# Two more pairs of column groups on Strassen's scheme, with two units each, in a matmul-bound decoder layer

## The chip, the cores and the metric

The kernel runs on one core of a Trainium2 chip. The time is that of one execution on the device, in microseconds (us). PE is the matmul engine, PEld its weight loads, DVE, ACT and POOL the vector, scalar and GpSimd engines, SP the engine whose queue issues the transfers.

## The reference

One decoder layer for 256 tokens of width 2048, in float32:

```python
h = rmsnorm(x, norm_mix_g)
u = h @ w_in                      # 12288 columns: c, b, xa, za, q, f, iv, og (1024 each), ga, gb (2048 each)
ya = b * conv3(c * xa) * silu(za)
o = hgrn2_chunked(silu(q), (1 - lb) * sigmoid(-f), iv, log_f)
yb = rmsnorm_per_head(o) * silu(og)
m = sigmoid(ga) * (ya @ w_a_out) + sigmoid(gb) * (yb @ w_b_out)
x = x + m @ w_o
x = x + sigmoid(rmsnorm(x) @ w_ple_gate) * (p @ w_ple_proj)
out = rmsnorm(x)
```

## The kernel before

Every projection is cut into groups of 512 output columns, and a group's 2048 input rows into eight chunks of 256. Tokens lie in two tiles of 128. The activations (`hT`, `mT`, `x1T`) stand on PE as stationary operands, split into a high and a low part (`xh`, `xl`), and the weights stream: PE makes three products per pair of tiles (`xh` with `whi`, `xh` with `wlo`, `xl` with `whi`), so a chunk of one group is 12 matmuls of 128x512.

A step is one such chunk. For each step ACT copies the loaded weights (`raw`, 128x1024) to `whi` (line 166) and DVE subtracts that from `raw` to make `wlo` (line 167); both are called the split here. Weights come in units of 1 MB through three `raw` buffers, and splits run three steps ahead of PE into four buffer pairs. In some stages more pairs stand ready: the table `MORE` names, per stage, tiles of other pools that are free then (`inner`: two, `outer`: two, `gates`: one), and `ahead` counts them.

Some groups are computed in pairs. A pair's program is a tuple such as `INNER` or `OUT`: `(0, 4)` is two steps, chunks 4 and 5 of the pair's first group; `(1, 4)` the same of the second; `(2, 3)` chunk 3 of both; `("S", 1)` is a **unit**: chunk 1 of both groups as one 2x2x2 block product by Strassen's scheme, in four steps (parts 0 to 3) of 6, 3, 6 and 6 matmuls. A unit needs sums of the weights, which DVE makes in place in `raw` (`combine_weights`, lines 181, 184 and 185), a split of the 512-wide third sum (part 1, here the half split), and sums of the activations, the forms (`forms`, lines 777 to 785). Its products land in four extra PSUM banks (`s`), and `sums` (line 845 is its `add`) puts these and the four plain banks (`g`) together when the last unit is done, so group 0 of a pair is finished before the pair ends if its own plain chunks stand early in the program.

The order of the groups: four of `w_ple_proj` (PP); for the first half of the columns f, then q with iv as a pair (QV, `FRONT`, 2 units), og, c, xa, za, b; for the second half f, q, then iv with og as a pair (VG, `INNER`, 3 units), c, xa, za, b; four pairs ga and gb (`OPENING` 2 units, `GATES` 4 each), each followed by its groups of `w_a_out` and `w_b_out`; `w_o` as a pair of groups 0 and 1 (OO, `OUT`, 3 units) and groups 2 and 3 alone; `w_ple_gate` as group 0 alone, groups 1 and 2 as a pair (GP, `LATE`, 3 units) and group 3 alone.

Behind its last matmul each group has an epilogue, a generator that `advance()` moves by one yield per step, so its operations stand in the engines' queues between the splits. `ep_f` scales the forget gate's logits, turns them through DRAM and a DVE transpose (line 354), takes two sigmoids, scales them by `oml` and `lbm` in eight 128x256 pieces on DVE (lines 407 and 414), and later takes logarithms on ACT and a scan on DVE (line 434). `ep_o` adds an output group to `x`, turns it, and makes the next operand `x1T` and, for the pair's groups, the gate's forms. `gated` applies the last gate. The scheduler of the build may move matmuls within what the waits allow; the queues of the other engines are in order.

Of the kernel before, what the change touches and what calls it, by code (L numbers as in the profile page):

```python
# [55 lines left out]
def hybrid_kernel(ctx, tc, xT, x, pT, prm, gfin, masks, w_in, w_a, w_b, w_o, w_pg, w_pp, out):  # L56
# [28 lines left out]
    def nm(s):  # L85
        uid[0] += 1
        return f"{s}_{uid[0]}"
# [86 lines left out]
    def combine_weights(pos):  # L174

        b = load(pos).rearrange("p i (k c) -> p (i k) c", k=2)
        pool, tag, n = ("tmp2", "t2", 2) if more(pos) in ("gates", "last") else ("tmp3", "t2", 1)
        if more(pos) in ("inner", "first"):
            pool, tag, n = "tmp1", ("both", "aoff")[unit_of[pos] // 2 % 2], 1
        t2 = half[unit_of[pos]] = pools[pool].tile([P, CW], F32, tag=tag, bufs=n, name=nm("t2"))  # L180
        nc.vector.tensor_tensor(  # L181
            out=b[:, 0:4:3, :], in0=b[:, 0:3:2, :], in1=b[:, 3:4, :].to_broadcast([P, 2, CW]), op=ALU.subtract
        )
        nc.vector.tensor_tensor(out=t2, in0=b[:, 2, :], in1=b[:, 0, :], op=ALU.add)  # L184
        nc.vector.tensor_tensor(out=b[:, 1, :], in0=b[:, 1, :], in1=t2, op=ALU.subtract)
# [27 lines left out]
    for gi, (kind, j, w, g, op, *program) in enumerate(groups):  # L213
# [4 lines left out]
        for n, (u, c) in enumerate(program[0]):  # L218
# [21 lines left out]
    gates, late = of_kind("GG"), of_kind("PG")[0]  # L240

# [11 lines left out]
    last = range(gates[-1] + 1, closing + 1)  # L253
    outer = range(closing + 6, of_kind("O")[-1] + 1)
    tied.append(range(last[0] - 4, outer[-1] + 1))
    inner = [of_kind(kind) for kind in ("QV", "VG")]
    inner = range(inner[0][0] - 3, inner[0][-1] + 1), range(inner[1][0] - 6, inner[1][-1] + 1)

    def more(pos):

        return "gates" if pos in gates else "last" if pos in last else "outer" if pos in outer else "first" if pos in g0 else "inner" if any(pos in at for at in inner) else None

# [132 lines left out]
    def ep_f(j, psum):  # L395
# [9 lines left out]
        for h in range(4):  # L405
            s = slice(h * T, (h + 1) * T)
            nc.vector.tensor_scalar(
                out=sg[:, s], in0=sg[:, s], scalar1=one[:, h : h + 1], scalar2=low[:, h : h + 1],
                op0=ALU.mult, op1=ALU.add,
            )  # L410
        yield
        for h in range(4):
            s = slice(h * T, (h + 1) * T)
            nc.vector.tensor_scalar(
                out=kT[:, s], in0=sn[:, s], scalar1=one[:, h : h + 1], scalar2=None, op0=ALU.mult
            )
        yield
# [406 lines left out]

    def forms_of_m():

        joined = sorted(c for u, c in OUT if u == "S")
        raws = []
# [5 lines left out]
        for j in range(0, len(joined), 2):  # L834
            chunks = joined[j : j + 2]
            r = raws[j // 2].rearrange("p (u k t) -> p u k t", u=2, k=2)[:, : len(chunks)]
            made = lambda: tuple(
                pools["tmp2"].tile([P, 1024], F32R, tag=f"Sx{j}{x}", bufs=1, name=nm("Sm"))[:, : 512 * len(chunks)] for x in "hl"
            )
            yield from forms("mT", made, r, chunks)  # L840
            for _ in range(3):
                yield

    def add(out, x, y):
# [153 lines left out]
    def ep_gates_late(j, e, left):  # L998
        def then(q, g):
            gate = gated(j + q, g, [g[:, A], g[:, B]])  # L1000
            next(gate)
            active.append(gate)
            if q == 0:
                load_projection(3)

# [240 lines left out]
    def ahead(pos):  # L1246

        at, n = more(pos + LEAD), 0
        while n < len(MORE[at]) and more(pos + LEAD + n + 1) == at and (at == "gates" or more(pos + LEAD - 2 * n) == at):
            n += 1  # L1250
# [68 lines left out]
    for pos, (gi, c) in enumerate(steps[:last_group]):  # L1319
        kind, j, w, g, opname, *program = groups[gi]  # L1320
        nch = w.shape[2]
        if kind == "PG" and j == 0 and c == 0:
            close_pool("outer")
# [25 lines left out]
        if pos == FORMS:  # L1349
            active.append(first_forms())  # L1350
            step(active[-1])
        if pos == inner[1][0] - 8:
            third = [
# [19 lines left out]
        if program:  # L1373
# [4 lines left out]
            if c == (min(n for n, (u, _) in enumerate(program) if u == "S"), 0) and kind not in ("G0", "OO"):  # L1378
                active.append({"GG": ep_pair, "GP": ep_gates_late, "QV": ep_inner, "VG": ep_inner}[kind](j, banks, left))
            pair_products(c, program, opname)  # L1380
            ask_ahead()
            if 0 <= pos - TOKENS < 4:
                load_tokens(pos - TOKENS)
            if not joint[pos] or c[1] % 2:
# [14 lines left out]
            if kind == "GP" and c in ((1, 1), (3, 1)):  # L1399
                load_projection(1 + c[0] // 2)  # L1400
            continue
# [14 lines left out]

        if kind == "PG" and j == 0 and c < 2:
            advance()
# [4 lines left out]
        if kind != "PG" or j or c >= 2:  # L1423
            advance()
        if pos == gates[-1] - 9:
            active.append(forms_of_m())
            step(active[-1])
        if kind == "O" and c == 1:
            residual(j)
        if kind == "O" and j == 2 and c == 4:  # L1430
            load_gfin()
        if kind == "PG" and c == 4:
            load_projection(j)
        if c == nch - 1:
# [106 lines left out]
```

## Time and profile before

| what | us |
|---|---|
| median of 3 runs | 808.21 (807.93 to 808.41) |
| the profiled execution | 809.07 |
| its span, first to last instruction | 807.3 |
| PE busy in it | 798.0 |
| DVE busy in it | 685.1 |
| ACT busy in it | 492.1 |

The granted clock of PE is 0.996 on average. A matmul's row lasts longer than the distance to the next row's start, since matmuls are pipelined; what one costs is read from the starts. "Splits run ahead" is read by comparing the end of a `wlo` row with the start of the first matmul that reads it.

### The profile page before, as it was taken

How to read it: one execution, taken by the hardware profiler on the slowest of the kernel's cores; microseconds unless marked ns; L12 is line 12 of the kernel's file. 1: busy time of each engine (PE TensorE's matmuls, PEld its weight loads, DVE VectorE, ACT ScalarE, POOL GpSimd, SP SyncE). 2: the span in 40 equal slices, each digit the busy share in tenths (PEclk: the TensorE clock that was granted, in tenths of full speed). 3: DMA queues.
4: the chain of work that ended last, by engine and by line, in shares of the span. 5: the costliest groups of instructions: out<-in, count | busy, mean ns of one | idle time of the engine just before them, and what ended most of it. 6: DMA issues, size and time to landing. Idle time of an engine off the chain costs nothing.

```text
span 807.3 us, 11113 instructions
## 1 busy us (share of the span) xinstructions
PE 798.0 (99%) x4169; PEld 662.3 (82%) x4169; DVE 685.1 (85%) x798; ACT 492.1 (61%) x662; POOL 95.4 (12%) x74
## 2 busy tenths in 40 slices
PE   9999999999999999999999999999999999999995
PEld 7888888888888888888888888888888888887885
DVE  5968897966779987978998998998998988859995
ACT  6967565575656665586674564564565556746562
POOL 0000145300000054300001000000100000002032
PEclk9999999999999999999999999999999999999998
DMA  9899855747676755667584775775875669877542
GB/s 345 295 335 319 268 174 203 237 167 241 240 261 190 261 183 201 209 211 257 189 307 158 227 275 171 239 264 179 275 266 196 208 246 348 327 236 281 205 173 104
DMA packets 50309, 191.20 MB, mean 237 GB/s; under 512 B 5712, under 2 KB 15184, under 8 KB 36304
## 3 DMA queue, kind: packets, MB, share of 16 engines
q1 hardware_dynamic: 50112, 190.24, 68.4%
q8 instruction: 32, 0.52, 0.2%
q10 hardware_dynamic: 144, 0.26, 0.1%
q14 instruction: 21, 0.17, 0.1%
HBM read 175.80 MB, written 14.68 MB: 236 GB/s over the span
## 4 chain that ended last, share of the span: by engine, by line
PE 82%; DVE 10%; issue 2%; DMA 2%; ACT 2%; SPq 0%; POOL 0%; ACTq 0%; POOLq 0%; DVEq 0%
PE g L1258 48%; PE g L1280 25%; PE s L1280 6%; DVE wlo L167 5%; DMA raw<-in_w_pg 2%; ACT whi L166 1%; DVE raw L181 1%; DMA raw<-in_w_o 1%; PE s L1258 1%; PE s L504 1%; DVE t L845 1%; PE s L1131 1%; DVE t L184 1%; DVE t L1017 0%; DVE t L354 0%
## 5 line engine op out<-in xcount | busy, mean ns | idle before, releaser
L167 DVE TENSOR_TENSOR wlo<-raw,whi 128x1024 fp32r<-128x1024 f32 (+1 forms) x320 | 390.2, 1243 | 92.2 <-ACT whi L166 89.4
L166 ACT ACTIVATE whi<-raw 128x1024 fp32r<-128x1024 f32 (+1 forms) x320 | 325.8, 1047 | 175.8 <-PE g L1258 98.3
L1258 PE MATMUL g<-whi,xl 128*128 128x512 f32 (+1 forms) x464 | 177.1, 382 | 0.3 <-DVE xl L311 0.3
L1258 PE MATMUL g<-whi,xh 128*128 128x512 f32 (+1 forms) x464 | 177.4, 383 | 0.0
L1258 PE MATMUL g<-wlo,xh 128*128 128x512 f32 (+1 forms) x464 | 177.1, 382 | 0.0
L1280 PE MATMUL g<-whi,xl 128*128 128x512 f32 x316 | 122.9, 389 | 0.0
L1280 PE MATMUL g<-wlo,xh 128*128 128x512 f32 x316 | 122.9, 389 | 0.0
L1280 PE MATMUL g<-whi,xh 128*128 128x512 f32 x316 | 122.6, 389 | 0.0
L1258 PEld LDWEIGHTS g<-whi,xl 128*128 128x128 f32 x464 | 87.2, 188 | 17.6 <-DVE xl L311 0.8
L1258 PEld LDWEIGHTS g<-whi,xh 128*128 128x128 f32 x464 | 87.2, 188 | 17.0 <-ACT xh L310 0.3
L1258 PEld LDWEIGHTS g<-wlo,xh 128*128 128x128 f32 x464 | 87.3, 188 | 16.8
L166 ACT ACTIVATE whi<-t 128x512 fp32r<-128x512 f32 x25 | 15.8, 632 | 92.1 <-DVE t L184 92.1
L1280 PEld LDWEIGHTS g<-whi,xl 128*128 128x128 f32 x316 | 59.3, 188 | 12.4
L1280 PEld LDWEIGHTS g<-whi,xh 128*128 128x128 f32 x316 | 59.3, 188 | 12.3
L1280 PEld LDWEIGHTS g<-wlo,xh 128*128 128x128 f32 x316 | 59.3, 188 | 12.3
L927 POOL TENSOR_TENSOR t<-ga,gb 128x512 f32<-128x512 f32 x6 | 10.6, 1790 | 188.0 <-issue 118.1
L181 DVE TENSOR_TENSOR raw<-raw 128x1024 f32<-128x1024 f32 x25 | 31.5, 1261 | 0.6
L1258 PE MATMUL g<-whi,yaTh 128*128 128x512 f32 (+1 forms) x74 | 28.2, 388 | 0.0
L1258 PE MATMUL g<-wlo,yaTh 128*128 128x512 f32 (+1 forms) x74 | 27.9, 383 | 0.0
L1258 PE MATMUL g<-whi,yaTl 128*128 128x512 f32 (+1 forms) x74 | 27.9, 383 | 0.0
L1258 PE MATMUL g<-whi,mh 128*128 128x512 f32 x64 | 24.8, 391 | 0.1
L1258 PE MATMUL g<-whi,ml 128*128 128x512 f32 x64 | 24.9, 389 | 0.0
(309 smaller groups left out, 1117.0 us busy)
## 6 DMA issues: line engine op xcount, KB each, us to landing
raw<-in_w_in SPq DMA_DIRECT2D x68, 1024.0 KB, 5.0
raw<-in_w_in SPq DMA_DIRECT2D x37, 512.0 KB, 5.1
raw<-in_w_o SPq DMA_DIRECT2D x12, 1024.0 KB, 6.5
raw<-in_w_pg SPq DMA_DIRECT2D x12, 1024.0 KB, 6.4
raw<-in_w_in SPq DMA_DIRECT2D x38, 256.0 KB, 5.1
turn<-t SPq DMA_DIRECT2D x72, 128.0 KB, 2.8
t<-turn SPq DMA_DIRECT2D x18, 512.0 KB, 5.2
raw<-in_w_a SPq DMA_DIRECT2D x8, 1024.0 KB, 5.6
```

The source lines that it names most:

```text
L166: a = nc.scalar.activation(out=hi[:, s], in_=src[:, s], func=AF.Copy)
L167: v = nc.vector.tensor_tensor(out=lo[:, s], in0=src[:, s], in1=hi[:, s].bitcast(F32), op=ALU.subtract)
L181: nc.vector.tensor_tensor(out=b[:, 0:4:3, :], in0=b[:, 0:3:2, :], in1=b[:, 3:4, :].to_broadcast([P, 2, CW]), op=ALU.subtract)
L184: nc.vector.tensor_tensor(out=t2, in0=b[:, 2, :], in1=b[:, 0, :], op=ALU.add)
L504: nc.tensor.matmul(heads(bk)[r, h, c if at is None else slice(at, at + 32)], key(h)[:, r], query(h)[:, c], start=True, stop=True, tile_pos ...
L845: nc.vector.tensor_tensor(out=out, in0=x, in1=y, op=ALU.add)
L927: (nc.vector if j == 3 else nc.gpsimd).tensor_tensor(out=spread(m, t), in0=blocks(ga[:, s]), in1=blocks(gb[:, s]), op=ALU.add)
L1131: nc.tensor.matmul(wb[:m, :n], *ones, start=True, stop=True)
L1258: nc.tensor.matmul(psum, a, b, start=first and n == 0, stop=last and n == 2)
L1280: nc.tensor.matmul(banks[name], x, y[:, s], start=k == total[name] and i == 0, stop=k == 1 and i == 2)
```

## The change

Four things change in the order of work, and some places follow.

- Second half: f and q become a pair (FQ, `SECOND`, units on chunks 0 and 1). Its forms are those that QV made. The epilogue is `ep_second`.
- `w_o`: groups 2 and 3 become a pair (`CLOSE`, units on chunks 0 and 1). Its forms are made again from `m`, which is read back from DRAM (`forms_of_m`, called a second time with the pool `outer`).
- `w_ple_gate`: the pair is groups 0 and 1 instead of 1 and 2, with a new `LATE`; group 2 is alone.
- `ep_f` makes its eight scalings on ACT instead of DVE, in both halves.
- Buffers and order: VG gets three extra pairs (`wide`) instead of two, FQ two (`inner`), the output pair one (`outer`) instead of two; the stretches in which splits keep their place among the other operations (`tied`) now hold VG and reach to the gate's last unit; loads of x, of the final gain and of the kept projections move with their groups.

```diff
+SECOND = (0, 2), (0, 4), ("S", 0), (0, 6), ("S", 1), (1, 2), (1, 4), (1, 6)
+CLOSE = (0, 2), (0, 4), (0, 6), ("S", 0), (1, 2), ("S", 1), (1, 4), (1, 6)
-LATE = (0, 4), ("S", 0), (0, 6), ("S", 1), (2, 3), ("S", 2), (1, 4), (1, 6)
+LATE = ("S", 0), (2, 3), ("S", 1), (0, 4), ("S", 2), (1, 4), (0, 6), (1, 6)
...
-        elif (kind, j) in (("iv", 0), ("og", 1)):
+        elif (kind, j) == ("f", 1):
+            groups.append(("FQ", j, w_in, n, "hT", SECOND))
+        elif (kind, j) in (("iv", 0), ("og", 1), ("q", 1)):
             continue
...
-    groups += [("OO", 0, w_o, 0, "mT", OUT), ("O", 2, w_o, 2, "mT"), ("O", 3, w_o, 3, "mT")]
-    groups += [("PG", 0, w_pg, 0, "x1T"), ("GP", 1, w_pg, 1, "x1T", LATE), ("PG", 3, w_pg, 3, "x1T")]
+    groups += [("OO", 0, w_o, 0, "mT", OUT), ("O", 2, w_o, 2, "mT", CLOSE)]
+    groups += [("GP", 0, w_pg, 0, "x1T", LATE), ("PG", 2, w_pg, 2, "x1T"), ("PG", 3, w_pg, 3, "x1T")]
...
-        "outer": ((("outer", "whi0"), ("outer", "wlo0")), (("outer", "whi1"), ("outer", "wlo1"))),
+        "outer": ((("outer", "whi"), ("outer", "wlo")),),
...
+        "wide": (
+            (("tmp1", "X"), ("tmp1", "X")), (("tmp1", "a"), ("tmp1", "y")), (("tmp1", "og"), ("tmp1", "cv")),
+        ),
...
-    outer = range(closing + 6, of_kind("O")[-1] + 1)
-    tied.append(range(last[0] - 4, outer[-1] + 1))
+    outer = range(closing + 5, of_kind("O")[-1] + 1)
+    tied.append(range(last[0] - 4, last_unit("GP", LATE) + 3))
     inner = [of_kind(kind) for kind in ("QV", "VG")]
-    inner = range(inner[0][0] - 3, inner[0][-1] + 1), range(inner[1][0] - 6, inner[1][-1] + 1)
+    wide = range(inner[1][0] - 4, inner[1][-1] + 1)
+    inner = range(inner[0][0] - 3, inner[0][-1] + 1), range(of_kind("FQ")[0] - 2, wide[0])
+    tied.append(wide)
...
-            nc.vector.tensor_scalar(
-                out=sg[:, s], in0=sg[:, s], scalar1=one[:, h : h + 1], scalar2=low[:, h : h + 1],
-                op0=ALU.mult, op1=ALU.add,
+            nc.scalar.activation(
+                out=sg[:, s], in_=sg[:, s], func=AF.Identity, scale=one[:, h : h + 1], bias=low[:, h : h + 1]
             )
...
-            nc.vector.tensor_scalar(
-                out=kT[:, s], in0=sn[:, s], scalar1=one[:, h : h + 1], scalar2=None, op0=ALU.mult
-            )
+            nc.scalar.activation(out=kT[:, s], in_=sn[:, s], func=AF.Identity, scale=one[:, h : h + 1])
...
+    def ep_second(j, e, left):
+
+        def then(q, g):
+            after = (ep_q if q else ep_f)(j, [g[:, A], g[:, B]])
+            next(after)
+            active.append(after)
+
+        yield from sums(e, left, lambda: (t4(), t4()), then)
...
             if pos == closing:
                 finish()
                 third_part()
                 state["x1T"] = operand(big, "x", KT)
                 active.append(ep_out(j, banks, left))
+                step(active[-1])
+                active.append(forms_of_m(sorted(c for u, c in CLOSE if u == "S"), homes_of_m("outer", "Sm")))
                 step(active[-1])
...
+            if kind == "O" and c in ((0, 1), (1, 1)):
+                residual(j + c[0])
+            if kind == "O" and c == (2, 1):
+                load_gfin()
```

DVE's queue where the output groups end and the gate begins, before: the first five splits of the gate's group 0 (`raw_6100`, `raw_6158`, `raw_6237`), with what group 1 and group 2 of the output still had to do (`So1l` is a form, `xl` a part of `x1T`).

```order
L167 TENSOR_TENSOR wlo_6222<-raw_6100,whi_6221 128x1024
L785 TENSOR_TENSOR So1l_6206<-t_1100_6160,So1h_6205 128x512
L167 TENSOR_TENSOR wlo_6240<-raw_6100,whi_6239 128x1024
L167 TENSOR_TENSOR wlo_6256<-raw_6158,whi_6255 128x1024
L354 STREAM_TRANSPOSE t_1103_6183<-t_1089_6102 128x4x8x32
L845 TENSOR_TENSOR xs<-xs,g_6116 128x512
L311 SCALAR_TENSOR_TENSOR xl_5826<-t_1103_6183,prm_t,xh_5825 128x256 x4
L845 TENSOR_TENSOR xs<-xs,g_6117 128x512
L167 TENSOR_TENSOR wlo_6289<-raw_6158,whi_6288 128x1024
L167 TENSOR_TENSOR wlo_6311<-raw_6237,whi_6310 128x1024
```

The same place after: the first unit of the gate's pair (`raw_6221`), between the sums of the output pair (line 853 is `add` there, 169 the split, 183 to 187 the combination).

```order
L169 TENSOR_TENSOR wlo_6292<-raw_6221,whi_6291 128x1024
L853 TENSOR_TENSOR t_1130_6235<-t_1130_6235,s_6146 128x1024
L853 TENSOR_TENSOR xs<-xs,t_1129_6234 128x512
L183 TENSOR_TENSOR raw_6221<-raw_6221 128x2x512
L186 TENSOR_TENSOR t_1142_6295<-raw_6221 128x512
L187 TENSOR_TENSOR raw_6221<-raw_6221,t_1142_6295 128x512
L169 TENSOR_TENSOR wlo_6320<-t_1142_6295,whi_6319 128x512
L169 TENSOR_TENSOR wlo_6336<-raw_6221,whi_6335 128x1024
L853 TENSOR_TENSOR t_1130_6235<-t_1130_6235,g_6159 128x512
L853 TENSOR_TENSOR t_1130_6235<-t_1130_6235,g_6174 128x512
L169 TENSOR_TENSOR wlo_6369<-raw_6221,whi_6368 128x1024
```

What moved: the unit that used to come a whole plain group later now stands directly behind the output pair, among that pair's last sums.

ACT's queue around the sigmoids of the second half's forget gate, before: they stand in the value and output gate's first unit (`raw_2152`), with no scalings.

```order
L166 ACTIVATE whi_2210<-raw_2152 128x1024
L400 ACTIVATE t_367_2208<-t_366_2206 128x1024
L402 ACTIVATE t_366_2206<-t_366_2206 128x1024
L166 ACTIVATE whi_2240<-t_370_2214 128x512
L166 ACTIVATE whi_2260<-raw_2152 128x1024
```

After: they stand in that pair's second unit (`raw_2264`), with the query's sigmoids (line 379) and the eight scalings (416 and 422) ahead of the half split's copy.

```order
L168 ACTIVATE whi_2366<-raw_2264 128x1024
L409 ACTIVATE t_393_2304<-t_392_2302 128x1024
L379 ACTIVATE t_399_2327<-t_363_2141,r1r_615 128x512 x2
L411 ACTIVATE t_392_2302<-t_392_2302 128x1024
L416 ACTIVATE t_393_2304<-t_393_2304,lc_54_330,lc_55_331 128x256 x4
L422 ACTIVATE kT_2340<-t_392_2302,lc_55_331 128x256 x4
L168 ACTIVATE whi_2385<-t_408_2370 128x512
```

What moved: everything that the forget gate still needs from ACT before its logarithms now stands between the first copy of that unit and its second.

More of the change, by code (lines that the diff above doesn't have):

```diff
@@ L177, in combine_weights @@
         pool, tag, n = ("tmp2", "t2", 2) if more(pos) in ("gates", "last") else ("tmp3", "t2", 1)
-        if more(pos) in ("inner", "first"):
+        if more(pos) in ("inner", "wide", "first"):
             pool, tag, n = "tmp1", ("both", "aoff")[unit_of[pos] // 2 % 2], 1
@@ L239, in hybrid_kernel @@
     of_kind = lambda *kinds: [pos for pos, (gi, c) in enumerate(steps) if groups[gi][0] in kinds]
-    gates, late = of_kind("GG"), of_kind("PG")[0]
+    gates, late = of_kind("GG"), of_kind("GP")[0]
     def last_unit(kind, program):
@@ L823, in forms_of_x, with forms_of_m @@
             yield
-    def forms_of_m():
-        joined = sorted(c for u, c in OUT if u == "S")
+    def forms_of_m(joined, made):
         raws = []
@@ L836, in forms_of_m, with homes_of_m @@
             r = raws[j // 2].rearrange("p (u k t) -> p u k t", u=2, k=2)[:, : len(chunks)]
[L837 to L840, printed above, removed]
+            yield from forms("mT", lambda: tuple(z[:, : 512 * len(chunks)] for z in made(j)), r, chunks)
             for _ in range(3):
                 yield
+    def homes_of_m(pool, tag):
+        return lambda j: tuple(
+            pools[pool].tile([P, 1024], F32R, tag=tag.format(j) + x, bufs=1, name=nm("Sm")) for x in "hl"
+        )
     def add(out, x, y):
@@ L1248, in ahead @@
         at, n = more(pos + LEAD), 0
-        while n < len(MORE[at]) and more(pos + LEAD + n + 1) == at and (at == "gates" or more(pos + LEAD - 2 * n) == at):
+        while n < len(MORE[at]) and more(pos + LEAD + n + 1) == at and (
+            at == "gates" or more(pos + LEAD - 2 * n) == at or at == "wide" and n < 2
+        ):
             n += 1
@@ L1321, in hybrid_kernel @@
         nch = w.shape[2]
-        if kind == "PG" and j == 0 and c == 0:
+        if kind == "GP" and c == (0, 0):
             close_pool("outer")
@@ L1351, in hybrid_kernel @@
             step(active[-1])
-        if pos == inner[1][0] - 8:
+        if pos == wide[0] - 10:
             third = [
@@ L1383, in hybrid_kernel @@
                 load_tokens(pos - TOKENS)
-            if not joint[pos] or c[1] % 2:
+            if (not joint[pos] or c[1] % 2) and (kind, c[0]) != ("GP", 0):
                 advance()
@@ L1414, in hybrid_kernel @@
                         )
-        if kind == "PG" and j == 0 and c < 2:
-            advance()
         if pos >= FIRST:
@@ L1422, in hybrid_kernel @@
             load_tokens(pos - TOKENS)
-        if kind != "PG" or j or c >= 2:
-            advance()
+        advance()
         if pos == gates[-1] - 9:
-            active.append(forms_of_m())
+            active.append(forms_of_m(sorted(c for u, c in OUT if u == "S"), homes_of_m("tmp2", "Sx{}")))
             step(active[-1])
[L1428 to L1433, printed above, removed]
+        if kind == "PG" and c in (3, 6):
+            load_projection(j + c // 6)
         if c == nch - 1:
```

10 lines of the change are left out of this document (5 added, 5 removed).

## The prediction

> **What bounds the kernel now.** I read the page's busy times first, then PE's waits, then the timeline, which shows what one matmul costs.
>
> ```profile
> span 807.3 us, 11113 instructions
> PE 798.0 (99%) x4169; PEld 662.3 (82%) x4169; DVE 685.1 (85%) x798; ACT 492.1 (61%) x662; POOL 95.4 (12%) x74
> ...
> PE s L1131 <- PEq L1530: 0.8, 1, 0.8
> PE g L1258 <- DVE xl L311: 0.3, 1, 0.3
> ...
> 668.67 0.39 PE L1258 MATMUL g<-whi,mh 128*128 128x512 f32 x1
> 668.89 0.39 PE L1258 MATMUL g<-wlo,mh 128*128 128x512 f32 x1
> 669.12 0.39 PE L1258 MATMUL g<-whi,ml 128*128 128x512 f32 x1
> 669.58 0.50 PE L1258 MATMUL g<-whi,mh 128*128 128x512 f32 x1
> ...
> 732.04 0.40 PE L1280 MATMUL g<-whi,xh 128*128 128x512 f32 x1
> 732.79 0.73 PE L1258 MATMUL g<-whi,xl 128*128 128x512 f32 x2 [0.35 <-DVE xl L311]
> ```
>
> PE is busy 99% and its named waits come to 1.1 us: PE is the bound, almost everywhere. A row lasts 0.39 us, but the next one starts 0.22 to 0.23 us after it, so a matmul is worth **0.2267 us** of time, not 0.39. Where starts lie further apart, PE waited: 0.23 us at 669 and 0.52 us at 732. With some 0.4 us in smaller gaps beside these two I count 1.2 us of waits between 668 and 733. DVE, at 85%, is the nearest rival, and it isn't even over the stages:
>
> ```profile
> 196.40:238.60 42.20, 42.20 (x188) 34.94 (x187) 30.38 (x35) 23.55 (x28) 0.11 (x1) 1.00 0.81 280
> 238.60:281.70 43.10, 43.07 (x190) 35.38 (x189) 40.43 (x49) 28.22 (x33) 0.53 (x1) 1.00 0.61 207
> 620.00:668.70 48.70, 48.70 (x217) 40.32 (x216) 45.35 (x51) 25.68 (x28) 0.00 (x0) 1.00 0.64 218
> 668.70:712.50 43.80, 43.73 (x193) 35.92 (x192) 33.02 (x41) 29.01 (x45) 0.00 (x0) 1.00 0.93 337
> 712.50:776.60 64.10, 63.75 (x280) 52.21 (x280) 56.30 (x63) 40.60 (x56) 7.71 (x3) 1.00 0.68 238
> ```
>
> The columns are stretch, length, then busy time of PE, weight loads, DVE, ACT, POOL. The stages are forget and query of the second half; value and output gate; output groups 0 and 1; output groups 2 and 3; the gate's groups 0 to 2. Stages with Strassen units hold DVE at 88 to 94%; the plain stages (72% and 75%) are where it gets ahead again. The change makes the plain ones Strassen too.
>
> **What it removes.** A unit makes 21 matmuls where a plain chunk of two groups makes 24. Four more units save 12 x 0.2267 = **2.72 us**. The waits at 669 and 730 to 733 belong to orders that go (a single output group behind the pair; the gate's group 0 needing the last output group at once), so up to 1.2 us go with them.
>
> **What a unit costs DVE.** From the stage of value and output gate:
>
> ```profile
> 263.61 1.22 DVE L181 TENSOR_TENSOR raw<-raw 128x1024 f32<-128x1024 f32 x1
> 264.87 0.69 DVE L184 TENSOR_TENSOR t<-raw 128x512 f32<-128x512 f32 x1
> 265.59 0.69 DVE L185 TENSOR_TENSOR raw<-raw,t 128x512 f32<-128x512 f32 x1
> 266.34 0.69 DVE L167 TENSOR_TENSOR wlo<-t,whi 128x512 fp32r<-128x512 f32 x1
> 267.50 5.76 DVE L167 TENSOR_TENSOR wlo<-raw,whi 128x1024 fp32r<-128x1024 f32 x5 [0.46 <-ACT whi L166]
> ...
> 664.95 0.68 DVE L845 TENSOR_TENSOR t<-t,s 128x512 f32<-128x512 f32 x1
> 670.04 1.21 DVE L845 TENSOR_TENSOR t<-t,s 128x1024 f32<-128x1024 f32 x1
> ```
>
> Start to start, the combination is 2.73 us (263.61 to 266.34), a half split 0.60, a whole split 1.14 (five in 5.76, the last one's tail off). A unit is 2.73 + 0.60 + 3 x 1.14 = 6.75 us of DVE for 21 x 0.2267 = 4.76 us of PE; the plain chunk is 2.28 for 5.44. So each new unit adds 4.5 us to DVE and takes 0.68 from PE. A new pair also adds its sums, six adds at 0.60 and one at 1.13: 4.7 us.
>
> **Output pair and the gate's pair.** Now three stages with units follow each other (3, 2 and 3 units) with nothing plain between. Take DVE's queue of the new order from behind the split of the output pair's fourth step to the last split of the gate's step (0, 4). Its kinds, counted in that queue:
>
> ```profile
> 667.71 1.22 DVE L167 TENSOR_TENSOR wlo<-raw,whi 128x1024 fp32r<-128x1024 f32 x1
> ...
> 683.14 1.24 DVE L354 STREAM_TRANSPOSE t<-t 128x1024 f32<-128x1024 f32 x1
> ...
> 685.76 0.42 DVE L780 TENSOR_TENSOR t<-t 128x256 f32<-128x256 f32 x1 [0.27 <-ACT t L963]
> 686.16 0.42 DVE L777 SCALAR_TENSOR_TENSOR t<-t 128x256 f32<-128x256 f32 x1
> ...
> 714.13 1.68 DVE L311 SCALAR_TENSOR_TENSOR xl<-t,prm_t,xh 128x256 fp32r<-128x256 f32 x4
> ```
>
> 24 whole splits 27.3; 4 half splits 2.4; 4 combinations 10.9; 19 adds of 512 at 0.60 11.4; two of 1024 2.3; forms of m (four small ones of 0.34 to 0.45, one whole) 2.6; and for the three first output groups transposes (1.16 each), splits of x1 and its forms 4.9 + 3.7 + 2.9. Sum **68.4 us**. The row at 667.71 is the split at which the count starts; it ends at 668.9, so DVE ends at 737.3 if it never waits. PE, from 668.67, reaches that split after 186 + 21 + 24 + 21 + 12 = 264 matmuls, 59.9 us: at 728.5. DVE is 8.7 us late, and PE waits at least that long: it has no other split to use. In the old order DVE was busy 33 us in the first 44 of these.
>
> Gates in the queue add to it. The split before the sums waits for a transfer, an ACT copy and a buffer that PE frees (1.2 us); the forms wait for ACT's gains, 0.3 in the row at 685.76 and about 1.5 where splits of ACT stand behind them; behind each half split ACT must copy first, 0.46 in the row at 267.50, four times 1.8; and a combination, a transpose and four splits of x1 come right after that stretch (1.4). That makes about 6, or 15 in all. Bounds 8.7 and 15; I take **13.5**, nearer to the upper end, since every gate has its row.
>
> The moved transfers (m's 512 KB read again, the 1 MB of x for groups 2 and 3 sooner, the projections' reads) stand before weights on SP's queue; each is 1.5 to 3 us of the 337 GB/s that the fourth window shows. They hide behind DVE's lateness; without that cover the weights of the first unit would be the later ones by 1.5 us. One outer buffer pair less is in the 1.2 us above.
>
> **Forget and query, then value and output gate.** DVE gets 2 x 4.5 + 4.7 = 13.7 us, and the eight scalings that go to ACT take about 2.4 from it (four each in the L407 and L414 rows below). It had 11.8 + 2.7 = 14.5 us idle in the two windows, so DVE alone just fits. ACT does not:
>
> ```profile
> 235.75 1.06 ACT L400 ACTIVATE t<-t 128x1024 f32<-128x1024 f32 x1 [1.00 <-DMA raw<-in_w_in]
> ...
> 241.31 1.24 ACT L370 ACTIVATE t<-g,r1r 128x512 f32<-128x512 f32 x2
> ...
> 243.52 1.28 ACT L424 ACT_TABLE_LOAD   x1
> ...
> 205.75 1.69 ACT L310 ACTIVATE ybTh<-t,prm_t 128x256 fp32r<-128x256 f32 x4
> ...
> 77.91 1.38 DVE L407 TENSOR_SCALAR t<-t,lc,lc 128x256 f32<-128x256 f32 x4 [0.37 <-ACT t L400]
> ...
> 241.09 1.14 DVE L414 TENSOR_SCALAR kT<-t,lc 128x256 f32<-128x256 f32 x4
> ```
>
> In the new order two sigmoids (2.0), the query's two (1.2) and the eight scalings (2 x 1.65, by the L310 row) stand on ACT directly ahead of the copy of the half split of the second unit: 6.5 us. Counted from FQ's first matmul, the split that opens FQ's second unit ends at 16.2: PE frees its buffer's predecessor at 11, one split and ACT's four gains of yb follow, then DVE's four splits of yb. From there to the transpose that releases the sigmoids DVE's queue holds 35.6 us (16 whole splits, two combinations, two half splits with their 0.46, the sums, two transposes, four others), so the sigmoids start at 52.7. PE wants the half split after 261 matmuls, at 59.2; with ACT's 6.5 and its copy it comes 0.5 late. The copies behind it, then the table load and the logarithms (2.4), then the scan, a combination and a transpose on DVE make it up to 5.4 by the third unit. Bounds 0 (DVE alone) and 5.4; I take **4**. In the first half the same block lies where splits are over 2 us ahead, and I cost it at nothing; without that cover it would be 1 us.
>
> ```profile
> 651.70 0.63 ACT L166 ACTIVATE whi<-t 128x512 fp32r<-128x512 f32 x1 [4.26 <-DVE t L184]
> 652.43 5.80 ACT L166 ACTIVATE whi<-raw 128x1024 fp32r<-128x1024 f32 x6
> ```
>
> ACT sat 4.26 us before a half split while six copies stood behind it. [...] Could ACT pass a blocked copy, this stage's term would be 0 and not 4.
>
> **The sum.** The profiled execution took 809.07 us, its span 807.3. 809.07 - 2.7 - 1.2 + 13.5 + 4 = 822.7. The median of the runs is 0.86 lower than the profiled one: **822 us**.
>
> **Rivals.**
> - **Only DVE's bare sum counts**: ACT's block finds its 0.5 us, and the gates are hidden in each other. 809.07 - 3.9 + 8.7 - 0.86 = 813. For it: PE's new order uses the high halves of two or three steps before the low ones, which bridges short waits. Against it: low halves are what is late. 0.22.
> - **Faster: DVE keeps up.** 808.2 - 3.9 = 804.3. It decides in favour of the change when all new waits stay under 3.9 us, so DVE's 68.4 us would have to shrink below 64, some 6%. For it: DVE's total over 620 to 776.6 was 134.7 of 156.6 us and would be 154, which fits if the work could be spread. Against it: the queue puts it in front, and DVE's rows repeat to a few per cent. 0.07; and 0.03 for a tie.
> - **PE's clock falls too.** Single waits of up to 3 us come close together in the gate's first two units. In the trace the clock stays 1.00 through waits of 0.5 us and is 0.60 in the last slice, where PE is idle 7 us. If it fell twice for some 3 us, at half rate, 3 us more: 825, and with all gates 828. 0.10. [...]
>
> **How the numbers follow.** The forecast, both stages late by their gates, gives 817 to 825.5 and has 0.58; the others 0.22, 0.10, 0.07 and 0.03. The range of 8 in 10 goes from 811.5, below the bare sum, to 828. About 0.2% (1.6 us) can be told from no change here. Slower 0.90, within 0.03, faster 0.07.
>
> **What would show it.** PE's matmul count falls by 12 and its starts stay 0.227 us apart inside steps. PE's wait list names DVE (low halves) and ACT, with over 10 us in the stretch from the output pair's second unit to the gate's second, and a few in the value stage's second and third unit; DVE is at 95% or more from the output pair's first unit to the gate's step (0, 4). It would be wrong if DVE idles in that stretch, if PE's waits there sum to under 8 us, or if new waits stand elsewhere, above all on transfers of weights.

## The result, and the profile after

The changed kernel takes **831.89 us** (median of 4 runs, 831.03 to 832.56) beside 808.31 us (807.93 to 808.67) for the kernel before: ratio 1.0291, 95% interval 1.0273 to 1.0309. It is slower by 23.6 us. The forecast was 822, with a range up to 828: the sign was right, the size was not.

The page of the changed kernel, busy times. The profiled execution took 832.56 us.

```profile
span 830.6 us, 11170 instructions
PE 805.5 (97%) x4156; PEld 659.9 (79%) x4157; DVE 709.3 (85%) x821; ACT 506.2 (61%) x689; POOL 90.6 (11%) x74
```

PE's waits in the changed kernel, with what ended each (columns: who waits, for what, us in total, times, longest):

```profile
PE s L1297 <- ACT whi L168: 8.1, 6, 2.3
PE g L1297 <- ACT whi L168: 2.2, 7, 0.9
PE g L1275 <- DVE t L853: 2.0, 1, 2.0
PE g L1297 <- DVE wlo L169: 1.7, 3, 0.9
PE s L1297 <- DVE wlo L169: 1.6, 5, 0.7
```

Most waits end with an ACT copy (`whi`, line 168), not with DVE. That is often the last link only: at the output pair's second unit the copy of the half split itself waits for the combination on DVE (3.53 us in this row):

```profile
706.09 0.63 ACT L168 ACTIVATE whi<-t 128x512 fp32r<-128x512 f32 x1 [3.53 <-DVE t L186]
```

Windows tell more: the length of a stretch less its matmuls at 0.2267 us is what PE waited in it.

```profile
254.00:276.00 22.00, 18.11 (x70) 12.01 (x69) 16.08 (x17) 15.96 (x23) 0.53 (x1) 1.00 0.43 143
700.00:716.00 16.00, 11.07 (x40) 6.68 (x39) 14.25 (x17) 10.57 (x15) 0.00 (x0) 1.00 0.56 208
716.00:750.00 34.00, 29.50 (x111) 22.41 (x110) 32.77 (x43) 20.12 (x32) 0.70 (x1) 0.90 0.65 217
774.00:780.00 6.00, 4.05 (x18) 3.03 (x17) 4.87 (x6) 5.31 (x7) 0.00 (x0) 1.00 0.85 317
```

The stretches are the second and third unit of value and output gate (22 - 70 x 0.2267 = 6.1 us of waits), the second unit of the output pair (6.9), the first two units of the gate's pair (8.8) and the step behind that pair (1.9). DVE is busy 96% of the third stretch, 89% of the second and only 73% of the first. The third one's clock, 0.90, is another thing that was new.

I also summed, for both traces, by how much starts of matmuls lie further apart than 0.2267 us (gaps over 0.3 us). That gives the terms of the prediction as they came:

| term | predicted | measured |
|---|---|---|
| 12 matmuls fewer | -2.7 | -2.7 |
| waits of before that go | -1.2 | -0.6 |
| value and output gate | +4 | +6.1 |
| output pair's second unit to the gate's second | +13.5 | +16.2 |
| behind the gate's pair | 0 | +2.2 |
| forget gate of the first half | 0 | +0.5 |
| third units of output groups 0 and 1 and of the gate | 0 | +1.1 |
| sum | +13.6 | +22.8 (spans: +23.3) |

Some 3 us of the 16.2 are not waits but matmuls that start 0.43 us apart, at a granted clock of 0.50.

### The profile page after: what moved, and what is told of

It reads as the page before. It is cut to its first block, busy times and chain, and to the rows that moved or that the text cites. A ratio compares the mean times of both kernels' runs of the same rounds, so it can differ in the third digit from the quotient of the medians.

```text
span 830.6 us, 11170 instructions
## 1 busy us (share of the span) xinstructions
PE 805.5 (97%) x4156; PEld 659.9 (79%) x4157; DVE 709.3 (85%) x821; ACT 506.2 (61%) x689; POOL 90.6 (11%) x74
## 4 chain that ended last, share of the span: by engine, by line
PE 73%; DVE 13%; ACT 4%; issue 4%; DMA 4%; SPq 0%; ACTq 0%; POOLq 0%; POOL 0%; DVEq 0%
PE g L1275 42%; PE g L1297 23%; DVE wlo L169 6%; PE s L1297 5%; ACT whi L168 3%; DVE raw L183 1%; DMA raw<-in_w_pg 1%; DMA raw<-in_w_o 1%; DVE t L853 1%; DVE t L363 1%; DVE t L186 1%; DMA raw<-in_w_in 1%; PE s L1275 1%; PE s L510 1%; PE s L1146 1%
## 5 line engine op out<-in xcount | busy, mean ns | idle before, releaser
L169 DVE TENSOR_TENSOR wlo<-raw,whi 128x1024 fp32r<-128x1024 f32 (+1 forms) x324 | 397.5, 1253 | 78.0 <-ACT whi L168 75.2
L1275 PE MATMUL g<-whi,xh 128*128 128x512 f32 (+1 forms) x400 | 152.7, 382 | 2.0 <-DVE t L853 2.0
L1275 PE MATMUL g<-wlo,xh 128*128 128x512 f32 (+1 forms) x400 | 152.5, 381 | 0.0
L1275 PE MATMUL g<-whi,xl 128*128 128x512 f32 (+1 forms) x400 | 152.1, 381 | 0.0
L1297 PE MATMUL g<-whi,xh 128*128 128x512 f32 x368 | 143.2, 391 | 1.3 <-ACT whi L168 1.3
L1297 PE MATMUL g<-wlo,xh 128*128 128x512 f32 x368 | 143.6, 390 | 0.0
L1297 PE MATMUL g<-whi,xl 128*128 128x512 f32 x368 | 143.4, 390 | 0.0
L1297 PE MATMUL g<-wlo,mh 128*128 128x512 f32 x98 | 38.3, 390 | 0.5 <-DVE wlo L169 0.5
L1297 PE MATMUL g<-whi,mh 128*128 128x512 f32 x98 | 38.0, 392 | 0.7 <-ACT whi L168 0.4
L1297 PE MATMUL g<-whi,ml 128*128 128x512 f32 x98 | 38.0, 390 | 0.0
```

The source lines that it names most:

```text
L169: v = nc.vector.tensor_tensor(out=lo[:, s], in0=src[:, s], in1=hi[:, s].bitcast(F32), op=ALU.subtract)
L1275: nc.tensor.matmul(psum, a, b, start=first and n == 0, stop=last and n == 2)
L1297: nc.tensor.matmul(banks[name], x, y[:, s], start=k == total[name] and i == 0, stop=k == 1 and i == 2)
```

## The experiments

Every ratio is against the kernel before, run beside it on the same chip. Medians of before were 808.1 to 808.8.

### The parts by themselves

`part_fq` has of the diff what concerns f and q of the second half, with `ep_f` and the buffers of that stage. `part_out_gate` is the changed kernel without it. `part_out` keeps of that only the output pair (old `LATE`, group 0 of the gate alone), `part_gate` only the gate's new pair. In short:

```diff
 part_out_gate and the next two:
-        elif (kind, j) == ("f", 1):
-            groups.append(("FQ", j, w_in, n, "hT", SECOND))
 part_out, and part_fq:
-    groups += [("GP", 0, w_pg, 0, "x1T", LATE), ("PG", 2, w_pg, 2, "x1T"), ("PG", 3, w_pg, 3, "x1T")]
+    groups += [("PG", 0, w_pg, 0, "x1T"), ("GP", 1, w_pg, 1, "x1T", LATE), ("PG", 3, w_pg, 3, "x1T")]
 part_gate and part_fq:
-    groups += [("OO", 0, w_o, 0, "mT", OUT), ("O", 2, w_o, 2, "mT", CLOSE)]
+    groups += [("OO", 0, w_o, 0, "mT", OUT), ("O", 2, w_o, 2, "mT"), ("O", 3, w_o, 3, "mT")]
```

> The kernel before with the first part of the change alone: forget and query of the second half as a pair, the eight scalings on ACT, the extra buffers of that stage; output groups and gate as before. Stage theory (each stage pays for its own lateness, and the parts add up): in the changed kernel's trace this part costs 6.1 us of waits in the value and output gate and 0.6 in the first half, and saves 6 matmuls x 0.2267 = 1.4; so 808.3 + 5.3 = 813.6. Rival (the stage only looks late because the later stages hold it up, or the other way round): the waits in the value stage are gone, 807 to 808.

> The changed kernel without that part: forget and query plain, scalings on DVE; output groups 2 and 3 a pair, gate pair of groups 0 and 1. Stage theory: waits 0.5 + 0.6 + 7.1 + 4.7 + 4.3 + 0.6 in the output groups and the gate, 2.2 behind the gate's pair, less 1.2 that before had there and 6 matmuls (1.4): 808.3 + 17.4 = 825.7, and with the first part's +5.3 the sum is the whole change, +22.7 against 23.6 measured. Rival: the parts share their cost, sum off by more than 2.

> The kernel before with the output pair of groups 2 and 3 alone; the gate in its old order (group 0 plain, then the pair of 1 and 2). Volume theory (DVE's work of the output pair has to be done before the pair's second unit, whatever follows): the 7.1 us of waits at that unit stay, the plain gate group behind takes the rest; 808.3 + 7.1 + 0.7 - 0.7 = 815.4. Rival, adjacency (only three stages of units in a row are too much; either alone has a plain stage behind it to catch up): 808 to 810.

> The kernel before with the gate's pair on groups 0 and 1 alone; output groups 2 and 3 plain. The plain groups before it let DVE get ahead, but the last group's sums, transposes and splits of x1 fall into the pair's first units. Volume theory: half of the 9.0 us in the gate's units was backlog of the output pair, half is the last output group's epilogue; 4.5, plus 2.2 behind the pair, less 0.8: 808.3 + 5.9 = 814. Adjacency: only the 2.2 behind the pair stays: 808 to 810.

| kernel | median us (range) | ratio, 95% interval |
|---|---|---|
| part_fq | 814.05 (812.95 to 814.26) | 1.0065 (1.0053 to 1.0077) |
| part_out_gate | 823.45 (822.77 to 824.43) | 1.0186 (1.0173 to 1.0199) |
| part_out | 821.31 (820.83 to 822.10) | 1.0163 (1.0150 to 1.0176) |
| part_gate | 817.28 (812.82 to 819.27) | 1.0104 (1.0082 to 1.0125) |

The first part costs 5.9 us, the second 15.3; together 21.2 of 23.6. The parts nearly add up; what is missing, 2.4 us, is just beyond the 2 us that the rival of `part_out_gate` asked for. 1.7 of it is one place: the wait behind the gate's pair was 0.57 us without the first part and 2.23 with it. Both theories failed on `part_out` and on `part_gate`. The second unit of `part_out` lost nearly what it loses in the changed kernel (13 us with 31 matmuls in a window of its trace: 6.0 beside 6.9), so adjacency is not the cause there. But the plain gate group behind it then stood still, for a reason that neither named. PE's rows of `part_out`:

```profile
727.19 0.39 PE L1277 MATMUL g<-whi,xl 128*128 128x512 f32 x1
732.89 0.79 PE L1277 MATMUL g<-whi,xh 128*128 128x512 f32 x1 [5.31 <-ACT xh L316]
...
734.40 0.63 PE L1277 MATMUL g<-whi,xh 128*128 128x512 f32 x1
734.83 0.63 PE L1277 MATMUL g<-wlo,xh 128*128 128x512 f32 x1
```

A pair finishes both its groups at its end, so x1 of groups 2 and 3 comes late, and a plain gate group wants it from its fifth chunk on: one wait of 5.3 us. The rows behind it start 0.427 us apart, not 0.227. The gate's new order, which asks for groups 2 and 3 last, removes this wait and pays for it in its own units; by itself it costs 9.1 us, beside the output pair only 2.1. In the trace of `part_gate` (815.41 us) the first unit lost 4.4 us, 1.4 of them to starts 0.43 us apart, and the group behind the pair 2.6; its slower executions, up to 819.27 us, have no trace.

### Forget gate: which engine, or which place

`scal_dve` puts the scalings of `ep_f` back on DVE in the changed kernel. `fq_lag` is `part_fq` with the transpose eight yields later, and the first half's scalings on DVE.

```diff
 fq_lag:
-        sn = yield from turned(fl, 4 if j else 6)
+        sn = yield from turned(fl, 12 if j else 6)
```

> The changed kernel with the eight scalings back on DVE, nothing else. Order theory (what stands on ACT directly ahead of the half split's copy sets the wait): 3.7 us of ACT leave the block between the sigmoids and that copy, DVE stood idle 3.7 and 2.1 us there anyway; the value stage's waits fall from 6.1 to about 3, the first half's 0.6 goes: 832 - 3.5 = 828.5. Rival, DVE's volume: 2.4 us more for DVE in a stage that is late, 832 to 834.

> The kernel before with the forget and query pair alone (as part_fq), with the transpose of the second half's forget gate eight yields later, so that sigmoids, scalings, logarithms and scan stand behind the splits of the third unit of value and output gate; the first half's scalings back on DVE. The work of each engine is that of part_fq. Order theory (the 6.4 us of waits come from this block standing inside the second and third unit, whichever engine it is on): they fall to under 1 us, and the 6 saved matmuls show: 808.1 - 1.4 + 0.5 = 807.2. Volume theory (DVE and ACT have too much to do in this stage): the waits come back behind the third unit or in the next group: 811 to 814.

`scal_dve` took 832.93 us (829.08 to 834.40), ratio 1.0306 (1.0289 to 1.0323): not told apart from the changed kernel. In its trace the first half's waits went, as expected, but those of the value stage fell only from 6.4 to 5.3 us, so the expectation that this block costs less on DVE failed. `fq_lag` took **807.51 us** (807.05 to 808.27, 11 runs), ratio 0.9981 (0.9972 to 0.9990): faster than before, and by the 0.2% that six matmuls are worth. Some 0.7 of the 6.5 us between `part_fq` and `fq_lag` are the first half's waits, which are gone with its scalings on DVE. The stage in `part_fq`, then in `fq_lag`:

```profile
254.00:276.00 22.00, 18.10 (x69) 12.02 (x69) 15.94 (x17) 15.96 (x23) 0.53 (x1) 1.00 0.45 144
```

```profile
236.00:282.00 46.00, 46.00 (x205) 38.09 (x204) 41.35 (x43) 32.37 (x42) 1.55 (x4) 1.00 0.68 230
```

205 matmuls at 0.2267 fill the 46 us: no wait is left in it, and 0.5 us stands just behind it, at 282.4, in a plain step. The work that DVE and ACT have to do for this block is the same. ACT's queue in the changed kernel shows what had stood in the way:

```profile
250.08 1.06 ACT L409 ACTIVATE t<-t 128x1024 f32<-128x1024 f32 x1 [4.16 <-DVE t L363]
251.05 1.32 ACT L379 ACTIVATE t<-t,r1r 128x512 f32<-128x512 f32 x2
252.27 1.04 ACT L411 ACTIVATE t<-t 128x1024 f32<-128x1024 f32 x1
253.22 2.06 ACT L416 ACTIVATE t<-t,lc,lc 128x256 f32<-128x256 f32 x4
255.19 1.69 ACT L422 ACTIVATE kT<-t,lc 128x256 f32<-128x256 f32 x4
256.79 0.61 ACT L168 ACTIVATE whi<-t 128x512 fp32r<-128x512 f32 x1
...
259.32 1.28 ACT L430 ACT_TABLE_LOAD   x1
...
261.77 2.94 ACT L168 ACTIVATE whi<-raw 128x1024 fp32r<-128x1024 f32 x3
```

The half split's copy at 256.79 is behind 6.7 us of the forget gate, the copies at 261.77 behind 2.4 us more, and DVE's splits wait for each. In `fq_lag` the forget gate's rows stand behind ACT's copies for the third unit, from 267.68 on, ahead of those of plain chunks.

### DVE's volume from the output pair to the gate

Three kernels change DVE's work in this stretch, or its place. `less_sums` and `short_comb` leave work out, as their expectations say.

```diff
 late_turn:
-        turn = turned(x1, 6 if j == 1 else 2)
+        turn = turned(x1, 6 if j == 1 else 8 if j == 0 else 2)
 less_sums, for groups 0 and 1 (sums of the pair, adds to x):
-        add(gb[:, A], gb[:, A], e[6])
-        add(both, both, e[5]...)
-        add(gb[:, A], gb[:, A], e[0, 1])
-        add(gb[:, B], gb[:, B], e[1, 1])
-            add(d, d, psum[t])
 short_comb, in combine_weights:
+        if pos < of_kind("O")[0]:
             nc.vector.tensor_tensor(out=b[:, 0:4:3, :], ...)
```

> The changed kernel with the transpose of output group 0 six yields later, so that its transpose, forms and low parts (5.5 us of DVE) stand behind the splits of the output pair's second unit and not ahead of its combination. DVE's work up to the gate's second unit is the same. Volume theory (PE's waits from 700 to 750 us are DVE's queue up to the gate's units, 72.8 us against 59.9 us of PE): the 7.1 us at the output pair's second unit fall to 2 or 3, what is gone comes back at the gate's first unit; 831 to 833. Local theory: 5 us less, 827.

> The changed kernel, with part of the sums of output groups 0 and 1 left out (four adds of their pair sums, the one over both tiles among them, and the four adds to x), so that group 0 and 1 of the output are not what the reference has: 5.3 us less for DVE, all of it 15 us and more ahead of the output pair's second unit. Volume theory (a backlog of DVE from the output pair's first step on is what PE meets later): 5.3 us less backlog, PE's waits from 700 to 750 us fall by 4 to 5: 827.5. Rival, local theory (the waits are set by what stands directly ahead of each half split): 831 to 832.

> The changed kernel, with the first of the three operations of the weight combination (1.25 us from start to start) left out in the two units of the output pair and the three of the gate's pair, so that their products are not the reference's: 5.0 us less for DVE up to the gate's second unit, with no work put on another engine. Volume theory (PE's waits from 700 to 750 us follow DVE's time one for one): 832 - 5.0 = 827. Rival (the waits are set by other links, the buffers, ACT's copies or the transposes): less than 2 us fall, 830 to 832.

| kernel | median us (range) | ratio, 95% interval |
|---|---|---|
| late_turn | 831.44 (828.65 to 835.04) | 1.0275 (1.0250 to 1.0301) |
| less_sums | 828.40 (828.05 to 832.14) | 1.0257 (1.0236 to 1.0278) |
| short_comb | 824.59 (823.76 to 826.44) | 1.0201 (1.0186 to 1.0216) |

The local theory falls with `late_turn`, whose time stays, although its executions spread over 6 us. The volume theory has the time right there and not the place: the first stretch lost less by 1.6 us and not by 4 to 5 (part of what it kept is the clock, 0.89 there), and nothing came back in the second. `short_comb` is the clearest in time: 6.25 us less of DVE, 7.3 us less time. The two windows of `late_turn`, then of `short_comb`:

```profile
700.00:716.00 16.00, 12.61 (x47) 9.36 (x46) 14.87 (x21) 12.96 (x19) 0.00 (x0) 0.89 0.83 305
716.00:750.00 34.00, 28.84 (x114) 21.83 (x114) 32.79 (x41) 19.05 (x31) 0.70 (x1) 0.95 0.56 189
```

```profile
700.00:716.00 16.00, 12.14 (x40) 7.72 (x39) 13.55 (x18) 11.72 (x16) 0.00 (x0) 0.89 0.54 197
716.00:750.00 34.00, 31.95 (x137) 25.08 (x136) 31.09 (x41) 20.45 (x33) 3.95 (x1) 1.00 0.79 269
```

PE waits 5.3 and 8.2 us in `late_turn` (6.9 and 8.8 in the changed kernel), 6.9 and 2.9 in `short_comb`. So the gate's first two units gained 5.9 us, for 5.0 us of DVE up to there; the wait behind the gate's pair (2.2) went too. The second unit of the output pair did not gain, although two of the five omissions are the output pair's. At this place ACT's copies sit 1.0 and 1.7 us for buffers that PE has to free, and the clock fell there (0.89, beside 1.00 in the changed kernel). One extra buffer pair less than before may be what makes the buffers the next limit; no run kept both pairs.

`short_comb` changes more than the volume. Without the first operation the build puts the rest of the combination earlier (for the gate's second unit from 725.46 on and not from 738.90), and with it ACT's copy of the half split. The gate's second unit in the changed kernel, where that copy stands behind the gains of an output group (line 319), then in `short_comb`, where it stands ahead of them (line 320 there):

```profile
740.78 1.71 ACT L319 ACTIVATE xh<-t,prm_t 128x256 fp32r<-128x256 f32 x4 [5.30 <-DVE t L363]
...
743.00 0.61 ACT L168 ACTIVATE whi<-t 128x512 fp32r<-128x512 f32 x1
```

```profile
729.35 0.61 ACT L168 ACTIVATE whi<-t 128x512 fp32r<-128x512 f32 x1
...
739.37 1.69 ACT L320 ACTIVATE xh<-t,prm_t 128x256 fp32r<-128x256 f32 x4
```

So it shows that the combinations' work on DVE costs this time, but not how much of it by volume and how much by place. For volume speak the length of the queue (70.1 us of DVE between 675.2 and 749.2, where PE's 264 matmuls need 59.9) and `less_sums`, which lies between the theories: about 3 us less for 5.3 us, with an interval that touches the changed kernel's. In its trace DVE idles 2.4 us for ACT's copies between 677 and 685, where it had no wait in the changed kernel, so some 3 us of the lead are left. Its profiled execution is its slowest, so its later stages are not read here.

`adds_on_pool` moves the adds to x from DVE to GpSimd:

```diff
-            add(d, d, psum[t])
+            nc.gpsimd.tensor_tensor(out=d, in0=d, in1=psum[t], op=ALU.add)
```

> The changed kernel with the eight adds of the four output groups to x on GpSimd, which is idle in this stretch, instead of DVE: 4.8 us less for DVE before the gate's second unit, at most 1.8 us each on GpSimd. Volume theory: PE's waits from 700 to 750 us fall by 4 to 5 us: 827.5. Rival (the chain of one output group's epilogue sets the end, or DVE's own instructions get longer beside GpSimd's): 831 to 834.

833.15 us (831.89 to 833.50), ratio 1.0294 (1.0278 to 1.0311): nothing gained. GpSimd's rows and DVE's of `adds_on_pool` show why:

```profile
679.18 1.39 POOL L963 TENSOR_TENSOR xs<-xs,t 128x512 f32<-128x512 f32 x1 [1.89 <-DVE t L853]
684.93 3.52 POOL L963 TENSOR_TENSOR xs<-xs,t 128x512 f32<-128x512 f32 x2 [4.36 <-DVE t L853]
```

```profile
679.02 0.41 DVE L786 TENSOR_TENSOR t<-t 128x256 f32<-128x256 f32 x1
679.36 1.50 DVE L787 TENSOR_TENSOR t<-t,t 128x256 f32<-128x256 f32 x1
...
685.38 4.17 DVE L169 TENSOR_TENSOR wlo<-raw,whi 128x1024 fp32r<-128x1024 f32 x2
```

The form of line 787 takes 1.50 us beside GpSimd's add and 0.42 otherwise; two splits take 4.17 us and 2.36 otherwise. For two adds (1.2 us) DVE lost 1.8 us, and over the whole kernel it is busy 710.9 us with eight adds fewer, beside 709.3. The rival holds.

### The clock, and the wait behind the gate's pair

`filler` puts matmuls with zeros where PE waits for the half splits of the gate's first two units; `late_order` changes the last chunks.

```diff
 filler, ahead of the product of the half split (8 in the first unit, 10 in the second):
+                for i in range(8 if n == 0 else 10):
+                    nc.tensor.matmul(banks[6], zeros, state["x1T"][0][:, 0:2, :] ...)
 late_order:
-LATE = ("S", 0), (2, 3), ("S", 1), (0, 4), ("S", 2), (1, 4), (0, 6), (1, 6)
+LATE = ("S", 0), (2, 3), ("S", 1), (0, 4), ("S", 2), (0, 6), (1, 4), (1, 6)
```

> The changed kernel, with 8 and 10 matmuls with zeros put ahead of the half split's product in the gate's first and second unit, where PE waits 2.05 and 2.48 us: 1.8 and 2.3 us of filling. In the changed kernel matmuls stand 0.427 us apart for 2 to 3 us behind each of these waits, against 0.227 otherwise, and the granted clock of these stretches reads 0.92 and 0.87. Clock theory: without the idle time the clock stays at 1.00, and the 1.5 us that each slow stretch costs go: 832 - 3 = 829. Rival: PE waits for splits there anyway, the clock costs nothing: 832; or the fillers push PE back: 833 to 834.

> The changed kernel, with the last plain chunks of the gate's group 0 ahead of those of group 1 ((0, 6) before (1, 4)). Theory: the wait of 2.2 us of the first plain gate group behind the pair is for the bank of group 0's first tile, which the sums read last but two splits after it is done; done 5.4 us sooner it is free in time: 832 - 2.2 = 829.7. Rival: the sums stand behind the splits of the next group anyway: 832.

PE's rows of the changed kernel at the gate's first unit show the slow stretch, and the two windows (changed kernel, `filler`) what became of it:

```profile
726.00 0.39 PE L1297 MATMUL g<-whi,xl 128*128 128x512 f32 x1
728.28 0.50 PE L1297 MATMUL s<-whi,So0h 128*128 128x512 f32 x1 [1.89 <-ACT whi L168]
...
731.42 0.63 PE L1297 MATMUL s<-whi,So0l 128*128 128x512 f32 x1
731.85 0.63 PE L1297 MATMUL g<-wlo,xh 128*128 128x512 f32 x1
```

```profile
725.00:750.00 25.00, 20.50 (x72) 14.96 (x71) 23.77 (x31) 16.15 (x25) 0.70 (x1) 0.86 0.58 191
```

```profile
725.00:750.00 25.00, 23.25 (x94) 16.73 (x93) 23.74 (x31) 16.16 (x25) 0.70 (x1) 1.00 0.58 190
```

With 18 fillers the clock stays at 1.00 in this window, and yet PE does 94 - 18 = 76 matmuls of the kernel in these 25 us and not 72: 0.9 us gained where 3 were expected. As much is lost again at the gate's third unit, whose waits are 1.4 us and not 0.55. The medians show nothing: 832.24 (830.97 to 832.43), ratio 1.0291 (1.0277 to 1.0305). DVE has the same work in both windows. The slow clock costs little there because PE would only wait longer for the next split. The trace of `filler` is not free of it, though: it has a slow stretch at the output pair's second unit (707.6 to 711.0; the clock of the whole execution is 0.994, beside 0.996 before), which that of the changed kernel has not (1.00 from 700 to 716).

`late_order` took 830.24 us (829.98 to 831.59), ratio 1.0273 (1.0259 to 1.0287), some 1.5 us less; the two intervals overlap, but the wait behind the pair is gone from its trace. In the changed kernel DVE's queue at this place reads:

```profile
775.09 2.36 DVE L169 TENSOR_TENSOR wlo<-raw,whi 128x1024 fp32r<-128x1024 f32 x2 [1.79 <-ACT whi L168]
777.37 0.68 DVE L853 TENSOR_TENSOR t<-t,g 128x512 f32<-128x512 f32 x1
```

The add at 777.37 frees the bank that group 2 needs; it had been due since the last product into it, but two splits that waited 1.79 us for ACT stood ahead. ACT in turn waited for a transfer of weights:

```profile
774.00 2.01 ACT L168 ACTIVATE whi<-raw 128x1024 fp32r<-128x1024 f32 x2 [2.15 <-DMA raw<-in_w_pg]
```

In `part_out_gate` the same copies waited 0.70 us for their weights (at 764.18), and PE 0.57 us behind the pair: this is most of the 1.7 us between the two. Why the transfer is later is not shown.

## Why the prediction was wrong

- **What bounds the kernel, and which parts cost**: right. PE's waits stand in the two stages that were named, behind half splits, and 12 matmuls are worth what was said.
- **Output pair and the gate's pair**: the mechanism and the queue were right (its operations are the 24 + 4 + 4 + 19 + 2 that were counted), the reading of it was not. The queue was to take 68.4 us and 4.8 for its gates; in the trace it runs from 676.41 (end of the output pair's fourth split) to 749.23 (last split of the step (0, 4)): 72.8:

```profile
675.19 1.22 DVE L169 TENSOR_TENSOR wlo<-raw,whi 128x1024 fp32r<-128x1024 f32 x1
...
744.60 5.77 DVE L169 TENSOR_TENSOR wlo<-raw,whi 128x1024 fp32r<-128x1024 f32 x5 [0.26 <-ACT whi L168]
```

  But the prediction failed at the step "DVE is 8.7 us late, and PE waits at least that long", with the count ended at (0, 4). PE takes up that split 2.4 us after it is done; its last wait is earlier, at the gate's second unit. Behind that point five splits follow each other on DVE (the row at 744.60; the fourth of them is the split of (0, 4) that I counted to), 1.14 us each, while PE needs 2.7 us for a plain step, so lateness shrinks by itself, but the waits have been paid. Another 0.85 us comes from the start: DVE ended that first split 1.08 us after PE's start of the pair, not 0.23. 72.8 + 1.08 + 2.4 - 59.9 = 16.4, which is what PE lost there, slow clock included (16.2 in the gaps of the table, the rest in smaller ones).
- **Forget and query**: the sum to the sigmoids was right (predicted at 52.7 us from the pair's first matmul at 197.0, so at 249.7; the row is at 250.08), and so was the block. Its size was 6.1 and not 4, beyond the bound of 5.4: 2.1 us at the half split of the second unit (the copy came 1.3 us late, not 0.5, and the low part behind it 0.5 more), 1.6 at the copies behind the table load, 2.6 at the third unit, less the 0.3 that before had there. The cause of it, the block's place and not its engine, `fq_lag` showed.
- **"In the first half ... I cost it at nothing; without that cover it would be 1 us"**: the cover was too thin, 0.5.
- **Waits left out**: behind the gate's pair I looked for no new wait. The new `LATE` ends with (0, 6), (1, 6), so group 0 is done late, and its sums then stand behind the next splits, which wait for weights: 2.2 us, shown by `late_order`. "... new waits stand elsewhere, above all on transfers of weights" was one of the prediction's own signs of being wrong. Of the waits that were to go, that at 669 stayed (0.34 before, 0.56 after).
- **The rivals**: "PE's clock falls too" came as it was put. No row of before shows the two falls of some 3 us at half rate that its 825 adds; the changed kernel's trace has two stretches of 3.4 us at a granted clock of 0.50 (0.86 from 725 to 750), the first behind a wait of 2.05 us with matmuls close before and behind. Its price did not come, by `filler`. "DVE keeps up" is refuted by every kernel with the output pair; it does hold for forget and query alone, once the block is moved.
- **The range**: its upper end, 828, let both stages be late by all gates that I had listed, and the clock fall twice. The places that I had costed at nothing are 3.8 us, about as much as the range missed by.

What stays open: 0.7 of the 2.4 us by which the two parts together cost more than their sum; how much of the 16.2 us is DVE's volume and how much the place of the half splits' copies; and the spread of some kernels. For `part_gate` it goes with the granted clock (812.82 us at 0.997, 819.27 at 0.991), and which of the two brings the other is not shown; for `late_turn` it does not (828.65 us at 0.992, 835.04 at 0.991).

## What to carry to other kernels

When a queue is longer than the work that it feeds, sum both up to **every** step and take the largest lateness on the way, not that at the end of the count; what the queue gains afterwards is not paid back. A block that an engine must do at some time costs by its place: the same sigmoids, scalings and logarithms cost 6 us between the splits of a unit and 0.5 us behind them, and moving them made forget and query's pair worth its matmuls (807.51 against 808.84 us). Before a step is moved to the end of a group, look at who needs the banks that it frees.

## What the runs showed of the hardware

- At full clock, the second matmul behind a wait started 0.33 to 0.34 us behind the first, not 0.227 (PE's rows of the changed kernel, waits of 0.34 to 2.11 us, where no other wait came between the two), so each of these waits cost 0.1 us beside itself:

```profile
778.11 0.50 PE L1275 MATMUL g<-whi,xh 128*128 128x512 f32 x1 [1.95 <-DVE t L853]
778.45 0.40 PE L1275 MATMUL g<-wlo,xh 128*128 128x512 f32 x1
778.69 0.40 PE L1275 MATMUL g<-whi,xl 128*128 128x512 f32 x1
```

- In the slow stretches of the changed kernel and of `part_out` matmuls of 128x512 start 0.427 us apart, 1.88 times 0.227. Those of the gate's first two units in the changed kernel lasted 3.4 us at a granted clock of 0.50 (729.9 to 733.3 and 743.6 to 747.0), that of `part_out` twice as long (731.9 to 738.7, from within its wait of 5.3 us on; 0.76 from 726 to 740). The length of a single wait did not tell whether one followed: in the changed kernel it did behind a wait of 2.05 us (to 728.28), and behind one of 2.11 us (to 778.11) the clock stayed at 1.00, as it did behind the waits of 1.0 to 1.3 us in the value stage.
- In `adds_on_pool` DVE's form of line 787 (128x256, both inputs in SBUF) took 1.50 us beside a GpSimd add, and 0.42 in the changed kernel; an add with an input in PSUM kept its 0.68 us (676.04, beside GpSimd's add from 675.22 to 677.28), and a split that had started ahead of that add kept its 1.22 us (674.91).
